# w_out as a Strassen product, x added by accumulating DMAs, eleven of gate_up's first products ahead

## The chip, the cores and the metric

One core of one Trainium2 chip runs the kernel. The metric is the device time of one execution in microseconds (us); the numbers shown are medians over runs. The profile beside it is one execution taken by the hardware profiler.

## The reference

One layer of a streaming encoder on x of 1024 tokens by 1024 channels, all in float32. What matters here, cut down:

```python
h = rmsnorm(x, norm_mix_pre)
proj = einsum("bsd,dn->bsn", h, w_in)            # q k v f, conv inputs, two gates
...                                              # branch A: gated short convolution
...                                              # branch B: forgetting attention, 8 heads
merged = sigmoid(gate_conv) * ya_d + sigmoid(gate_attn) * yb_d
m = einsum("bsd,de->bse", merged, w_out)         # 1024 x 1024 weights
x = x + rmsnorm(m, norm_mix_post)
h = rmsnorm(x, norm_ffn_pre)
gu = einsum("bsd,df->bsf", h, w_gate_up)         # 1024 x 5632
g, u = split(gu, 2)
f = einsum("bsf,fd->bsd", silu(g) * u, w_down)   # 2816 x 1024
x = x + rmsnorm(f, norm_ffn_post)
```

## The kernel before

**A product of matrices.** Each float32 operand is split into a rounded part `hi` (a copy on ScalarE, ACT) and the rest `lo` (a subtraction on VectorE, DVE). `mm3` then issues three matmuls, hi·hi, hi·lo and lo·hi, each 128 by 128 weights with 512 moving columns, into one PSUM bank. A `strassen` product takes a block of two by two blocks with seven block products instead of eight (Winograd's form): its sums of blocks are made by DVE on both operands, its results are combined by DVE from the banks `b1`, `b2`, `b3` into `c11`, `c12`, `c21`, `c22`. One block product here is 4 k-steps by 3 = 12 matmuls, a whole job is 84.

**The stages, in order.** Norm of x; the projections with w_in as 18 Strassen jobs; the attention, with the rest of branch A between its steps; branch B (`pbb`, 16 groups of 12 matmuls, whose results are gated and added into `um`, the transposed activations); w_out; gate_up as 22 Strassen jobs (f = 0 to 21); the down product (`pd`), the last norm and the output.

**w_out.** It is a plain product. `woh`/`wol` hold the whole weight matrix, split while `pbb` runs. `e_mm(st)` takes one tile of 128 tokens: two halves of 512 output columns, 8 k-steps, 3 matmuls each, into the bank `pm`. `e_norm(st)` follows one tile behind: sum of squares on ACT, a row scale `rms_scale` (six small DVE and ACT steps), the gain `gpo`, the addition of x (tile `xt`, loaded by the SP queue) on DVE, a POOL DMA that stores the new x in `x2_dram`, a second sum of squares and scale, the gain `gpr`, and eight transposes `tp` of 128x128 on TensorE (PE) that put the tile back into `um`.

**The first products.** Gate_up's Strassen jobs need activations of all tokens, but their first product and a half (`b1` over A11·B11 and A12·B21) only those of the first four tiles. So for f below `NPRE` these are done ahead (`f_first`): four of them before the last e_norm, the others between the groups of `h2_sums`, which form the sums of activations `hth` and `hch`. P1 and C11 are parked in `pre_dram` by POOL DMAs and loaded again (`c<-pre_dram`) when job f runs.

**What sets the order.** A scheduler places every instruction on its engine's queue at build time from dependences and priorities; the queues run in order. `strict` names engines whose instructions keep the order of the program. Pools have few buffers (4 `hi`, 3 `lo`, 3 `raw`, 1 `s4`, 2 `s4h`/`s4l`), so a load or a split also waits for the last reader of its buffer. A helper on line 76 records nearly all instructions, so rows are told apart by their tiles, not by lines; in the profile PE's bank of any Strassen product reads `b`, and its operands `hi`, `lo`, `s4h`, `s4l` and the activations' names.

Of the kernel before, what the change touches and what calls it, by code (L numbers as in the profile page):

```python
# [39 lines left out]
NPRE = 7  # L40
# [6 lines left out]
def block_kernel(  # L47
# [69 lines left out]

    def copy(o, a):
        nc.scalar.activation(o, a, AF.Copy)
# [16 lines left out]
    stat.tile([P, 24], F32, name="pad", bufs=1)  # L136
# [11 lines left out]
    pre_dram = [dpool.tile([2, P, NC], F32, name=f"pre_dram{f}") for f in range(NPRE)]  # L148
    ri_dram = [dpool.tile([2, S], F32, name=f"ri_dram{j}") for j in range(4)]
    sg_dram = [dpool.tile([2, P, S], F32, name=f"sg_dram{d}") for d in range(8)]  # L150
# [59 lines left out]
    av, av_close = pool("av")  # L210
    psa, psa_close = pool("psa", 4, space=PSUM)
# [82 lines left out]
    def turn(st, hn):  # L294
# [11 lines left out]
        if st < 4:  # L306
            if hraw is None:
                hraw = av.tile([P, KT, NC], F32, name="hraw")
# [36 lines left out]
        return [(b12h, b12l), bot], rest  # L345

# [37 lines left out]
    for st in range(ST):  # L384
# [5 lines left out]
        if st + 3 == ST:  # L390
            ax_close()
            w0, w0_close = pool("w0", side="right")
            r0 = w0.tile([P, KT, P], F32, name="r0")
            h0, l0 = (w0.tile([P, KT, P], F32R, name=n) for n in ("h0", "l0"))
            nc.sync.dma_start(r0, win[:, C_Q : C_Q + P].rearrange("(k p) m -> p k m", p=P))
            split(h0, l0, r0)
# [3 lines left out]

    av_close()
# [110 lines left out]
    def strassen(w, hb, psp, tmp, p1=None):  # L512
# [8 lines left out]
        prod(b2, w["S2"], hb[T2], True)  # L521
        c12 = t_(tmp, "c12")
# [301 lines left out]

    zts = {}
# [3 lines left out]
    for ij, (kind, j, _, _) in enumerate(jobs):  # L829
        if ij == 2:  # L830
            logf_pre = forget_sums()
# [55 lines left out]
        else:  # L887
# [286 lines left out]
    wo_pool, wo_close = pool("wo", side="right")  # L1174
    woh = wo_pool.tile([P, KT, D], F32R, name="woh")
    wol = wo_pool.tile([P, KT, D], F32R, name="wol")
# [25 lines left out]
    ha_pool, ha_close = pool("ha")  # L1202
    hah = ha_pool.tile([P, 2, 4, NC], F32R, name="hah")
    hal = ha_pool.tile([P, 2, 4, NC], F32R, name="hal")
    fp, fp_close = pool("f", 2)
    ep, ep_close = pool("e")
    gpo = bcast_row(norm_mix_post[0], ep, name="gpo")
    gpr = bcast_row(norm_ffn_pre[0], ep, name="gpr")

    def e_mm(st):  # L1210
        ss = slice(st * P, (st + 1) * P)
        mh, ml = hi_t(), lo_t()
        split(mh, ml, um[:, :, ss])
        pm = []
        for n in range(2):
            ns = slice(n * NC, (n + 1) * NC)
            ps = psm.tile([P, NC], F32, tag="mm", name="pm")
            for k in range(KT):
                mm3(
                    ps, (mh[:, k, :], ml[:, k, :]), (woh[:, k, ns], wol[:, k, ns]),  # L1220
                    k == 0, k == KT - 1,
                )
            pm.append(ps)
        return pm

    def load_xt(st):
        xt = z_tile("xt")
        nc.sync.dma_start(xt, x2d[st * P : (st + 1) * P, :])
        return xt

    def e_norm(st, pm):
        ss = slice(st * P, (st + 1) * P)
        xt = xts.popleft()
        if st + 1 < ST:
            xts.append(load_xt(st + 1))
        tt = ep.tile([P, D], F32, tag="t", name="tt", bufs=1)
        s2 = st_tile("s2", 2)
        for n in range(2):
            ns = slice(n * NC, (n + 1) * NC)
            nc.scalar.activation(tt[:, ns], pm[n], AF.Square, accum_out=s2[:, n : n + 1])  # L1240
        ssq = st_tile("ssq")
        add(ssq, s2[:, 0:1], s2[:, 1:2])
        rs = rms_scale(ssq)
        for n in range(2):
            ns = slice(n * NC, (n + 1) * NC)
            nc.vector.scalar_tensor_tensor(
                tt[:, ns], pm[n], rs, gpo[:, ns], op0=ALU.mult, op1=ALU.mult
            )
        add(xt, xt, tt)
        nc.gpsimd.dma_start(x2_dram[ss, :], xt)  # L1250
        ssq = st_tile("ssq")
        nc.scalar.activation(tt, xt, AF.Square, accum_out=ssq)
        rs = rms_scale(ssq)
        nc.vector.scalar_tensor_tensor(tt, xt, rs, gpr, op0=ALU.mult, op1=ALU.mult)
        for q in range(2):
            tp = psm.tile([P, 4, P], F32, tag="mm", name="tp")
            for k in range(4):
                kt = 4 * q + k
                nc.tensor.transpose(tp[:, k, :], tt[:, kt * P : (kt + 1) * P], ident)
            copy(um[:, 4 * q : 4 * q + 4, ss], tp)  # L1260
# [4 lines left out]
    def f_first(f):  # L1265
# [355 lines left out]
```

## Time and profile before

| what | value |
|---|---|
| time, median of 3 runs | 1350.11 us (1350.0 to 1350.78) |
| the profiled execution: its time, its span | 1350.04 us, 1348.2 us |
| PE busy, share of the span | 1328.5 us, 99% |
| DVE, ACT, POOL busy | 932.3, 535.2, 127.2 us |
| granted TensorE clock | 9 of 9 tenths in each of 40 slices |
| DMA moved | 186.36 MB, 138 GB/s |

The busy time of an engine is summed over its instructions' rows; for PE the rows' ends are modelled and neighbouring rows overlap, so the distance between starts tells its pace. The span is the time from the first to the last instruction of the profile. The execution's own time is 1.8 us longer than its span.

### The profile page before, as it was taken

The page shows a single profiled execution, that of the slowest core. Times are in us where ns is not written, and L with a number is a line of the kernel's source. Part 1 is how long each engine was busy: PE and PEld are TensorE (multiplying, and loading weights), DVE is VectorE, ACT ScalarE, POOL GpSimd, SP SyncE. Part 2 cuts the span into 40 slices and gives each one's busy share as a digit, 9 for nine tenths or more (in the row PEclk, how much of TensorE's full clock was granted, in tenths as well). Part 3 has the DMA queues.
Part 4 walks back from the last instruction along what each step waited for, and adds up shares of the span by engine and source line. Part 5 has one row for each costly group of instructions (what it writes and reads, how often), then busy time and mean ns, then how long its engine had stood idle before and what let it go on. Part 6 is the DMA issues. An engine that isn't in the chain of part 4 may idle for free.

```text
span 1348.2 us, 17709 instructions
## 1 busy us (share of the span) xinstructions
PE 1328.5 (99%) x6753; PEld 1098.9 (82%) x6753; DVE 932.3 (69%) x1445; ACT 535.2 (40%) x851; POOL 127.2 (9%) x252
## 2 busy tenths in 40 slices
PE   9999999999999999999999999999999999999997
PEld 7978888888887778788887788888888888888886
DVE  6974668754556766775669698776677766677585
ACT  6642222243345756613547232223222323444452
POOL 0001000011112112000002121100111011000000
PEclk9999999999999999999999999999999999999999
DMA  5332422333325444362235565332323236965541
GB/s 189 118 109 86 126 70 71 105 123 109 102 82 192 158 142 165 126 218 79 94 110 175 170 200 167 102 100 80 117 102 118 93 111 240 361 235 196 161 164 63
DMA packets 153256, 186.36 MB, mean 138 GB/s; under 512 B 9409, under 2 KB 106753, under 8 KB 153170
## 3 DMA queue, kind: packets, MB, share of 16 engines
q1 hardware_dynamic: 138434, 136.67, 32.4%
q0 software_dynamic: 14736, 48.54, 9.3%
q8 instruction: 53, 0.87, 0.3%
q14 instruction: 33, 0.27, 0.1%
HBM read 136.10 MB, written 49.09 MB: 137 GB/s over the span
## 4 chain that ended last, share of the span: by engine, by line
PE 58%; DVE 3%; DMA 2%; issue 1%; ACT 1%; POOL 0%; DVEq 0%; SPq 0%; POOLq 0%; ACTq 0%
PE b L76 28%; PE pd L76 15%; PE pm L76 5%; PE pbb L76 3%; PE pba L76 2%; PE po L76 1%; PE tps L76 1%; PE sp L76 1%; DMA pre_dram<-s 1%; DMA tk<-in_w_down_dram 1%; DVE tt L76 0%; DVE lo L76 0%; PE tp L76 0%; DMA pre_dram<-c 0%; ACT tt L76 0%
## 5 line engine op out<-in xcount | busy, mean ns | idle before, releaser
L76 DVE TENSOR_TENSOR c<-c,b 128x512 f32<-128x512 f32 x195 | 132.9, 682 | 91.4 <-PE b L76 72.3
L76 DVE TENSOR_TENSOR lo<-raw,hi 128x1024 fp32r<-128x1024 f32 (+1 forms) x93 | 112.0, 1204 | 83.1 <-PE b L76 68.8
L76 ACT ACTIVATE hi<-raw 128x1024 fp32r<-128x1024 f32 (+1 forms) x100 | 101.7, 1018 | 127.9 <-PE b L76 75.7
L76 PE MATMUL b<-hth,hi 128*128 128x512 f32 x352 | 137.3, 390 | 0.0
L76 PE MATMUL b<-hth,lo 128*128 128x512 f32 x352 | 137.0, 389 | 0.0
L76 PE MATMUL b<-htl,hi 128*128 128x512 f32 x352 | 136.9, 389 | 0.0
L76 ACT ACTIVATE hi<-sx 128x1024 fp32r<-128x1024 f32 x41 | 43.5, 1062 | 220.9 <-PE b L76 195.3
L76 PEld LDWEIGHTS b<-hth,hi 128*128 128x128 f32 x352 | 66.1, 188 | 14.6 <-DVE c L76 1.0
L76 PEld LDWEIGHTS b<-hth,lo 128*128 128x128 f32 x352 | 66.1, 188 | 13.8
L76 PEld LDWEIGHTS b<-htl,hi 128*128 128x128 f32 x352 | 66.1, 188 | 13.7
L76 DVE TENSOR_TENSOR lo<-sx,hi 128x1024 fp32r<-128x1024 f32 x41 | 50.2, 1224 | 33.6 <-PE b L76 31.4
L76 PE MATMUL b<-hah,hi 128*128 128x512 f32 x176 | 69.0, 394 | 1.2 <-ACT c L76 1.2
L76 PE MATMUL b<-hal,hi 128*128 128x512 f32 x176 | 68.5, 389 | 0.0
L76 PE MATMUL b<-hah,lo 128*128 128x512 f32 x176 | 68.4, 390 | 0.0
L76 DVE TENSOR_TENSOR sx<-raw 128x512 f32<-128x512 f32 x78 | 53.6, 688 | 19.1 <-DMA raw<-in_w_in_dram 9.0
L76 PE MATMUL pd<-hi,lo 128*128 128x512 f32 x160 | 62.3, 389 | 0.0
L76 PE MATMUL pd<-hi 128*128 128x512 f32 x160 | 62.0, 390 | 0.0
L76 PE MATMUL pd<-ghi 128*128 128x512 f32 x148 | 57.6, 390 | 0.0
L76 PE MATMUL pd<-glo,ghi 128*128 128x512 f32 x148 | 57.6, 389 | 0.0
L76 PE MATMUL pd<-ghi,glo 128*128 128x512 f32 x148 | 57.6, 389 | 0.0
L76 PE MATMUL b<-hT34h,hi 128*128 128x512 f32 x136 | 53.0, 390 | 0.4 <-DVE c L76 0.4
L76 PE MATMUL b<-hT34h,lo 128*128 128x512 f32 x136 | 52.9, 389 | 0.0
(368 smaller groups left out, 3359.9 us busy)
## 6 DMA issues: line engine op xcount, KB each, us to landing
raw<-in_w_gate_up_dram SPq DMA_DIRECT2D x51, 512.0 KB, 3.8
raw<-in_w_in_dram SPq DMA_DIRECT2D x35, 512.0 KB, 3.8
a_dramS<-um POOLq DMA_DIRECT2D x44, 256.0 KB, 2.8
a_dramA<-um POOLq DMA_DIRECT2D x33, 256.0 KB, 2.8
xt<-in_x_dram SPq DMA_DIRECT2D x16, 512.0 KB, 4.3
sg<-sg_dram SPq DMA_DIRECT2D x32, 256.0 KB, 4.6
graw<-a_dramS SPq DMA_DIRECT2D x14, 512.0 KB, 4.0
sg_dram<-c POOLq DMA_DIRECT2D x24, 256.0 KB, 2.3
```

Of the source, the lines that this page charges most:

```text
L76: ins = getattr(self.engine, name)(*args, **kw)
```

## The change

It has five parts.

1. **w_out by Strassen.** The tokens are taken as four pairs of tiles; each pair is a product of two by two blocks with 7 x 12 matmuls. For all four pairs the first product and a half come first (`first`, `second`; kept in `keeps`), then for each pair the other five products (`strassen`), `e_norm(i)` for two tiles at once, and `e_turn(i)`, its 16 transposes, placed in PE's queue behind the first product (S2) of pair i+2 for pairs 0 and 1, and within `f_first(0)` and `f_first(3)` for pairs 2 and 3. `sums` makes the sums of activations, those of pair 0 on POOL.
2. **w_out's weights.** Their seven block operands are formed and split during projection jobs 1 to 16 (`wo_load`: four loads of 128x128, four subtractions, one split of 128x896 each), stored in `wo_dram` by DMAs on ACT's queue one job later, and loaded as `x0` to `x5` (512 KB each, 28 loads) in `pbb` and after it.
3. **Gate_up's weights for the first products.** In projection jobs 1 to 11 one 128x1024 block each is loaded, split and stored in `pw_dram` (`pw_load`). `f_first` loads its `hi` and `lo` from there and splits nothing.
4. **NPRE 7 to 11.** Eleven first products are done ahead.
5. **x added by DMA.** `e_norm` writes the scaled tile into `x2t`; a POOL DMA adds x to it (`accum_op=add`), then an SP DMA stores it in `x2_dram`, and the second sum of squares reads it.

```diff
-NPRE = 7
+NPRE = 11
+    def pinned(call, *names):
+        was, strict[0] = strict[0], names
+        call()
+        strict[0] = was
...
-    def strassen(w, hb, psp, tmp, p1=None):
+    def strassen(w, hb, psp, tmp, p1=None, after=None):
...
         prod(b2, w["S2"], hb[T2], True)
+        if after is not None:
+            after()
         c12 = t_(tmp, "c12")
...
+    def wo_load(n):
+        k, c = divmod(n, 4)
+        r, h, l = w0_tiles()
+        for slot, (row, half) in enumerate(((k, 1), (k, 0), (4 + k, 0), (4 + k, 1))):
+            c0 = half * NC + c * P
+            nc.sync.dma_start(r[:, slot], wout_d[row * P : (row + 1) * P, c0 : c0 + P])
+        def cut():
+            for o, a, b in ((4, 0, 1), (5, 3, 4), (6, 3, 0), (7, 2, 5)):
+                sub(r[:, o], r[:, a], r[:, b])
+            split(h[:, 1:], l[:, 1:], r[:, 1:])
...
+    def pw_load(f):
+        r = t0_.tile([P, S], F32, tag="cb", name="rg", bufs=2)
+        h, l = (t0_.tile([P, S], F32R, tag="p", name=n, bufs=2) for n in ("hg", "lg"))
+        nc.sync.dma_start(kblk(r), kmaj(wgu[:, f * P : (f + 1) * P]))
...
     for ij, (kind, j, _, _) in enumerate(jobs):
+        for _, store in side.pop(ij - 1, ()):
+            pinned(store, "scalar")
+        if 0 < ij < len(jobs) - 1:
+            side[ij] = [wo_load(ij - 1)] + ([pw_load(ij - 1)] if ij <= NPRE else [])
...
+        for cut, _ in side.get(ij, ()):
+            pinned(cut, "vector", "scalar")
...
             sg = sg_tile()
             nc.sync.dma_start(sg, sg_dram[d][1, :, ns])
+            load_wo(*loads.pop(0))
...
-            if n == 0:
-                wr = flat(raw_t())
-                nc.sync.dma_start(wr, wout_d[d * P : (d + 1) * P, :])
-                split(woh[:, d, :], wol[:, d, :], wr)
+            if n and d == 1:
+                first_ops(0, [s4h_t(), s4h_t()], [s4l_t(), s4l_t()])
+                sums(0, s4_t())
...
+    def e_norm(i, c12, c21, c22):
+        qa, qb = qas[i], st2("qb")
+        for c, acc in ((c12, qb[:, 0:1]), (c21, qa[:, 1:2]), (c22, qb[:, 1:2])):
+            square(c, acc)
+        add(qa, qa, qb)
+        rs = scale2(qa)
...
+        for e, parts in enumerate((((n1, keeps[i][:, 1]), (n2, c12)), ((n1, c21), (n2, c22)))):
+            xt = xp[e]
+            for ns, c in parts:
+                nc.vector.scalar_tensor_tensor(
+                    xt[:, ns], c, rs[:, e : e + 1], gpo[:, ns], op0=ALU.mult, op1=ALU.mult
                 )
...
+            nc.gpsimd.dma_start(xt, x2d[rows_, :], accum_op=ALU.add)
+            nc.sync.dma_start(x2_dram[rows_, :], xt)
+            nc.scalar.activation(tt[e], xt, AF.Square, accum_out=ssq[:, e : e + 1])
+        rs = scale2(ssq)
...
-        add(xt, xt, tt)
-        nc.gpsimd.dma_start(x2_dram[ss, :], xt)
...
-    def f_first(f):
-        w, _ = prep_first(f_src(f)[0])
-        b1, p1 = strassen_first(w, hb, psm, fp)
+    def f_first(f, p1=None, after=None):
+        h1, l1 = hi_t(), lo_t()
+        for t, d in zip((h1, l1), pw_dram[f]):
+            nc.sync.dma_start(f32(flat(t)), d)
+        b1 = bank(psm, "b1")
+        prod(b1, (h1[:, LO], l1[:, LO]), hb[B11], True)
+        if after is not None:
+            after()
...
+    ops = rest_ops(0)
+    for i in range(PAIRS):
+        nxt = rest_ops(i + 1) if i + 1 < PAIRS else None
+        _, *cur = strassen(
+            ops, wob, psm, fe, keeps[i][:, 0], (lambda: e_turn(i - 2)) if i > 1 else None
+        )
+        e_norm(i, *cur)
...
+    f_first(0, p1_of(0), lambda: e_turn(2))
+    h2_sums(0)
+    f_first(1, p1_of(1))
+    h2_sums(1)
+    f_first(2, p1_of(2))
+    f_first(3, p1_of(3), lambda: e_turn(3))
...
+    for f in range(4, NPRE):
+        f_first(f)
```

**Where instructions stand now.** PE's queue at the first transposes of w_out's results. Before, the tile `tt_5835` (tokens 0 to 127) is turned behind all 48 matmuls of the next tile (`pm_5783` and `pm_5808`):

```order
L76 MATMUL pm_5808<-woh_5398,hi_5779 128x512
L76 MATMUL pm_5808<-wol_5399,hi_5779 128x512
L76 MATMUL pm_5808<-woh_5398,lo_5780 128x512
L76 MATMUL tp_5870<-ident_139,tt_5835 128x128 [waits DVE_49]
L76 MATMUL tp_5870<-ident_139,tt_5835 128x128 x3
L76 MATMUL tp_5876<-ident_139,tt_5835 128x128 x4
L76 MATMUL pm_5886<-woh_5398,hi_5882 128x512 [waits Activation_49]
```

In the changed kernel the same place is in pair 2: `b2_6524` is its S2, `tt_6351` and `raw_6121` are the two normed tiles of pair 0, `b3_6525` is pair 2's next product:

```order
L76 MATMUL b2_6524<-x2_5748,hi_6379 128x512 x2
L76 MATMUL b2_6524<-x2_5748,lo_6380 128x512
L76 MATMUL tp_6538<-ident_155,tt_6351 128x128 [waits DVE_49]
L76 MATMUL tp_6538<-ident_155,tt_6351 128x128 x3
L76 MATMUL tp_6544<-ident_155,tt_6351 128x128 x4
L76 MATMUL tp_6550<-ident_155,raw_6121 128x128 [waits DVE_49]
L76 MATMUL tp_6550<-ident_155,raw_6121 128x128 x3
L76 MATMUL tp_6556<-ident_155,raw_6121 128x128 x4
L76 MATMUL b3_6525<-x3_5749,hi_6383 128x512 [waits Activation_49]
```

Sixteen transposes now stand together, and in front of the rest of pair 2, where eight stood behind a whole tile.

ACT's queue in the same norm. Before, for the first tile: the sum of squares of the new x waits for DVE alone, and the copies from `tp` follow:

```order
L76 ACTIVATE tt_5835,s2_5836<-pm_5754 128x512 [waits PE_49]
L76 ACT_TABLE_LOAD
L76 ACTIVATE sq_5842<-va_5841 128x1 [waits DVE_49]
L76 ACTIVATE tt_5835,ssq_5856<-xt_5723 128x1024 [waits DVE_49]
L76 ACTIVATE sq_5859<-va_5858 128x1 [waits DVE_49]
L76 ACTIVATE hi_6203<-um_3496 128x1024 [waits PE_49,Activation_49]
L76 ACTIVATE um_3496<-tp_5870 128x4x128 [waits PE_49]
L76 ACTIVATE um_3496<-tp_5876 128x4x128 [waits PE_49]
```

In the changed kernel, for pair 0 (`DMASW` are semaphores of POOL's DMAs; `junk_6463` and `junk_6465` already belong to pair 1's norm):

```order
L76 ACTIVATE hi_6510<-um_3844 128x512 [waits PE_49]
L76 ACTIVATE hi_6510<-s3_6099 128x512
L76 ACTIVATE tt_6351,ssq_6354<-x2t_6352 128x1024 [waits DMASW3_49,DMASW7_49,DMASW2_49,DVE_49]
L76 ACTIVATE s4h_6520<-um_3844 128x512 [waits PE_49]
L76 ACTIVATE raw_6121,ssq_6354<-x2t_6353 128x1024 [waits DMASW3_49,DVE_49]
L76 ACTIVATE junk_6463,qb_6462<-c12_6407 128x512 [waits DVE_49,Activation_49]
L76 ACTIVATE sq_6366<-va_6365 128x2 [waits DVE_49]
L76 ACTIVATE hi_6514<-um_3844 128x1024 [waits PE_49]
L76 ACTIVATE junk_6465,qa_6105<-raw_6136 128x512 [waits DVE_49,Activation_49]
L76 ACTIVATE junk_6467,qb_6462<-c22_6421 128x512 [waits Activation_49]
L76 ACTIVATE um_3844<-tp_6538 128x4x128 [waits PE_49]
```

The squares of `x2t` wait for the accumulating DMAs, and pair 1's combining, squares and pair 3's splits stand between them and the transposes.

DVE's queue in a projection job. Before, the splits of the weights and the combining of the results:

```order
L76 TENSOR_TENSOR c12_2698<-c21_2682,b2_2684 128x512 [waits DMASW4_49,PE_49,Activation_49]
L76 TENSOR_TENSOR c22_2712<-c21_2682,b3_2685 128x512 [waits DMASW3_49,PE_49]
L76 TENSOR_TENSOR lo_2646<-raw_2643,hi_2645 128x1024 [waits PE_49]
L76 TENSOR_TENSOR lo_2656<-sx_2651,hi_2655 128x1024 [waits PE_49,Activation_49]
L76 TENSOR_TENSOR c22_2712<-c22_2712,b2_2684 128x512 [waits DVE_49]
```

In the changed kernel the sums and splits of w_out's weights (`r0`, `l0`) and of gate_up's (`lg`) stand in the same queue:

```order
L76 TENSOR_TENSOR r0_2431<-r0_2431 128x128 [waits DMAHW1_49]
L76 TENSOR_TENSOR s4l_2634<-s4_2631,s4h_2633 128x512 [waits Activation_49]
L76 TENSOR_TENSOR r0_2431<-r0_2431 128x128 [waits DMAHW4_49,DVE_49]
L76 TENSOR_TENSOR r0_2431<-r0_2431 128x128
L76 TENSOR_TENSOR r0_2431<-r0_2431 128x128 [waits DMAHW2_49,DVE_49]
L76 TENSOR_TENSOR c12_2666<-c21_2650,b2_2652 128x512 [waits PE_49]
L76 TENSOR_TENSOR c22_2680<-c21_2650,b3_2653 128x512 [waits PE_49]
L76 TENSOR_TENSOR l0_2433<-r0_2431,h0_2432 128x896 [waits DMAHW3_49,Activation_49]
L76 TENSOR_TENSOR lg_2440<-rg_2438,hg_2439 128x1024 [waits DMAHW7_49,Activation_49]
L76 TENSOR_TENSOR lo_2614<-raw_2611,hi_2613 128x1024 [waits PE_49]
L76 TENSOR_TENSOR c22_2680<-c22_2680,b2_2652 128x512 [waits DVE_49,PE_49]
```

Six instructions more stand in such a job, two of them ahead of the splits that PE needs next.

More of the change, by code (lines that the diff above doesn't have):

```diff
@@ L1226, in load_xt, with st2 @@
[L1226 to L1245, printed above, removed]
+    def st2(name, bufs=2):
+        return ep.tile([P, 2], F32, tag=name, name=name, bufs=bufs)
@@ new lines, in scale2, with square @@
+    def scale2(ssq):
+        return rms_scale(ssq, None, lambda n, w: st2(n), 2)
+    def square(src, acc):
+        junk = ep.tile([P, NC], F32, tag="junk", name="junk")
+        nc.scalar.activation(junk, src, AF.Square, accum_out=acc)
+    sx = wtile("sx", 1)
+    for i in range(1, PAIRS):
+        first_ops(i, hi_t(), lo_t())
+        sums(i, ep.tile([P, 4, P], F32, name="s3") if i == 3 else sx[:, 4 * i - 4 : 4 * i])
+    turned = []
+    qas = [st2("qa", PAIRS) for _ in range(PAIRS)]
+    b1s = {}
```

243 lines of the change are left out of this document (167 added, 76 removed).

## The prediction

> **What bounds the kernel.** I read the page's first two parts, then the chain of waits, then PE's rows at the stage that changes.
>
> ```profile
> span 1348.2 us, 17709 instructions
> PE 1328.5 (99%) x6753; PEld 1098.9 (82%) x6753; DVE 932.3 (69%) x1445; ACT 535.2 (40%) x851; POOL 127.2 (9%) x252
> L76 PE MATMUL b<-hth,hi 128*128 128x512 f32 x352 | 137.3, 390 | 0.0
> ```
>
> TensorE is the bound. But a matmul must not be priced at the 390 ns of its row: the rows overlap. The chain gives the pace, as long runs of matmuls with nothing between them:
>
> ```profile
> 567.59 43.52 PE pbb L76 x192
> 681.99 10.93 PE pm L76 x48
> 771.64 354.18 PE b L76 x1560
> ```
>
> 43.52 us / 192 and 354.18 / 1560 are both 0.227 us from start to start, and w_out's own 10.93 / 48 is 0.228. So a PE that never waits is paid by the number of matmuls at 0.2267 us, and what remains are its waits. From the end of the attention to the gate_up jobs these are few:
>
> ```profile
> PE b L76 <- DVE c L76: 2.1, 2, 1.5
> PE b L76 <- ACT c L76: 1.2, 1, 1.2
> PE tr L76 <- DVE ri L76: 0.7, 1, 0.7
> PE tp L76 <- DVE tt L76: 0.3, 1, 0.3
> ```
>
> These are the waits in 556 to 800 us: total, count, longest. `tr` belongs to the attention. The other 3.6 us are idle time after a modelled end; an interrupted pair of matmuls also loses the overlap of 0.39 - 0.227 = 0.16 us, which with two gaps of 0.2 us too small for the list makes about 4.6 us by starts.
>
> **Fewer matmuls.** The tile `pm` has three rows like this one, 384 matmuls:
>
> ```profile
> L76 PE MATMUL pm<-woh,hi x128: 389/389/481, 610.9 to 703.8; 128*128 128x512 f32 x128
> ```
>
> Four pairs by 7 products by 12 are 336. The first products of gate_up are only moved, and the 64 transposes stay. So 48 matmuls go: 48 x 0.2267 = 10.9 us (not 48 x 0.39 = 18.7).
>
> **Old waits that go.** The four waits above sit in front of code that is replaced: a norm tile late for its transposes, the last e_norm before f_first(4), the reload of P1 and C11 before the first gate_up jobs. I take all 4.6 us off and charge what is late next.
>
> **The norm of a pair, and its transposes.** This is the main new wait. The durations:
>
> ```profile
> L76 DVE SCALAR_TENSOR_TENSOR tt<-pm,r,gpo 128x512 f32<-128x512 f32 x14 | 9.9, 747 | 0.7
> L76 DVE SCALAR_TENSOR_TENSOR tt<-xt,r,gpr 128x1024 f32<-128x1024 f32 x7 | 9.0, 1285 | 0.2
> L76 DVE TENSOR_TENSOR sx<-um 128x512 f32<-128x512 f32 x1 | 0.7, 693 | 0.1
> L76 DVE TENSOR_SCALAR va<-ssq 128x1 f32<-128x1 f32 x14 | 2.2, 154 | 8.8 <-ACT tt L76 8.6
> L76 ACT ACTIVATE tt<-pm 128x512 f32<-128x512 f32 x14 | 8.2, 602 | 3.8 <-PE pm L76 3.8
> L76 ACT ACTIVATE tt<-xt 128x1024 f32<-128x1024 f32 x7 | 7.4, 1061 | 27.2 <-DVE xt L76 27.2
> L76 ACT ACTIVATION_READ_ACCUMULATOR tt<-pm 128x1 f32 x14 | 3.0, 213 | 0.0
> L76 ACT ACT_TABLE_LOAD x1 | 1.3, 1283 | 0.0
> ```
>
> Count from the last matmul of pair 0's fifth product. PE then has pair 1's 60 matmuls and pair 2's 12 of S2, 72 x 0.2267 = 16.3 us, until it stands at pair 0's transposes. Meanwhile DVE adds the last result (0.7), ACT squares the two last blocks (2 x 0.8) and loads a table (1.3), the scale takes six small steps of 0.15 to 0.2 us with their hand-overs (1.3), and two gains of 0.75 finish the first tile: POOL can issue at about 6.6 us, and for the second tile at 7.9. Landing takes L. Then ACT squares (1.06 + 0.18 us), but in the order of its queue: pair 3's split and pair 1's square stand in between (0.63 and 0.8), and DVE has pair 1's last addition and a split of 0.6 us ahead of the gains of 1.285 us. With L = 4.3 the second tile has landed at 12.2, is squared at 13.5, the scale (two engines, with 0.8 of pair 1's square and 1.3 of DVE's in between) ends at about 17.2, and the two tiles are ready at 18.6 and 19.9. PE waits from 16.3 to 18.6, turns eight blocks (0.9 us) and waits a little again: 2.5 us. The landing itself is nowhere in the trace of before, which has no accumulating DMA. The nearest rows:
>
> ```profile
> x_dram<-xt POOLq DMA_DIRECT2D x8, 512.0 KB, 2.9
> xt<-in_x_dram SPq DMA_DIRECT2D x16, 512.0 KB, 4.3
> DMA to landing us min/median/max: 2.9/2.9/7.3
> ```
>
> POOL's stores of the same 512 KB land in 2.9 us, the loads of the same rows of x in 4.3, and the slowest transfer of this tile took 7.3. An accumulation reads x as the load does, so I take 4.3, with 2.9 and 7.3 as ends. Per microsecond of L the wait grows by about one: 1.9 us (a floor, since the other work in both queues then sets it) to 5.5.
>
> The Trainium skill, "DMA: Bandwidth & Descriptors", section "Anatomy of one DMA — SWDGE (gpsimd) path", fits such a transfer as 2.0 us plus its bytes at 436 GB/s, which is an estimate of 3.2 us here; the 2.9 us of POOL's stores agrees. By it the four waits of this part would be about 2.5 us smaller in all and the sum 1341.0. That fit is for plain transfers, so I stay with the load's row.
>
> The same layout for the other pairs: pair 1's tiles are just in time (0.1; up to 3 at 7.3), pair 2's, turned in f_first(0), are late by 1.1 (0 to 4), pair 3's in f_first(3) by 1.7 (0.3 to 4.6). Pair 3's S4 product needs `c22` of an earlier bank released, behind four gains on DVE: 1.1 us (0 to 1.5). These are 6.5 us in all.
>
> **First products and their parking.** Eleven f_first issue 22 loads of 512 KB on SP; SP runs in order, and one load of f=7 stands behind raw loads that wait for DVE's sums. PE has 24 x 0.2267 = 5.4 us for each f_first, a load takes 3.8 in the row below, DVE nothing: 0.5 us (0 to 2).
>
> ```profile
> raw<-in_w_gate_up_dram SPq DMA_DIRECT2D x51, 512.0 KB, 3.8
> 745.55 4.80 DMA pre_dram<-c
> 751.27 3.07 DMA pre_dram<-s
> 756.68 0.47 PE L76 MATMUL b<-hch,s4h 128*128 128x512 f32 x1 [1.46 <-DVE c L76]
> ```
>
> The last three rows are the old case of the reload: POOL stores P1, waits, reloads, and PE's first S4 waits 1.46 us. In the new order the last f_first parks twice more just before the first job, and its `s4` is the buffer the job needs: the same wait, 1.5 us (0 to 2.2). The four jobs more that run with a reload cost nothing: in 772 to 900 us, where seven such jobs run, PE is never idle with DVE at 82%.
>
> **The projections.** Sixteen jobs get DVE work: four subtractions of 128x128 (between 0.15 us for 128x1 and 0.69 for 128x512; 0.3 by a straight line), a split of 128x896 (1.1) and, in eleven jobs, one of 128x1024 (1.22): 3.5 us. The cover is DVE's idle time, smallest in the conv jobs:
>
> ```profile
> core 0: us, PE busy (x) PEld busy (x) DVE busy (x) ACT busy (x) POOL busy (x), PEclk, DMA share, GB/s
> 147.00:166.10 19.10, 19.10 (x87) 15.73 (x86) 13.69 (x20) 5.42 (x7) 1.63 (x3) 1.00 0.58 167
> 261.90:281.00 19.10, 19.10 (x85) 15.79 (x85) 15.00 (x22) 7.33 (x9) 2.70 (x5) 1.00 0.47 152
> 772.00:900.00 128.00, 128.00 (x565) 105.57 (x564) 105.36 (x151) 37.23 (x47) 20.03 (x37) 1.00 0.45 146
> ```
>
> 15.0 + 3.5 = 18.5 of 19.1 us in the fullest, about 17.2 in the others: full, but under. A queue this full delays single splits that PE waits for; I take 0.4 us in all, and 4 as the upper end (0.5 in each of eight jobs). ACT has 12 us free per job; its four DMA issues (0.33 to 0.55 us on the other queues) wait for splits of a job before, so nothing stands behind them. In `pbb` the 28 loads replace eight splits; DVE and PE lose work or keep it: nothing.
>
> **The sum.** -10.9 (matmuls) - 4.6 (old waits) + 2.5 + 0.1 + 1.1 + 1.7 + 1.1 (pairs) + 0.5 + 1.5 (first products) + 0.4 (projections) = -6.6 us. The profiled execution took 1350.04 us, 0.07 below the median 1350.11, so the forecast is 1343.5. With no new wait at all it would be 1334.6; with L = 2.9, about 1340; with every wait of the pairs at its upper end, 1355.
>
> **Rivals.**
> (a) The turns are hidden: DVE and ACT are ahead of my layout, as in before, where of eight groups of transposes only one waits 0.3 us, and L is near 2.9. Then 2 to 4 us of waits remain: about 1338.
> (b) Slower: the accumulating DMA is slow. Each of the four turns gets a microsecond for each microsecond of L beyond 4.3, since POOL's landing stands on the chain of all of them: 6.6 us of gain are used up at L = 5.9, and 0.2% is lost at L = 6.6. At 7.3 the sum is 1355. For it: it reads and writes, and up to eight loads run beside it. Against it: the median rows, all under 5.
> By the Trainium skill, "TensorE: Matmul & The Clock Gate", section "Part 1: The HAM clock gate", an idle window of about 3.4 us halves the clock until some 3.4 us of work have passed. Then each gap longer than that would cost about 1.7 us more as an estimate; no gap of before is so long, and its clock is full throughout.
> (c) DVE saturates: the conv jobs' stall takes the upper end of 4 us, or more where a job's queue runs over. With 0.5 to 1 us in each of eight jobs the time is 1347 to 1351, no change.
>
> **How the numbers follow.** 0.2% of 1350 is 2.7 us, about what a measurement of this kernel can tell from no change. My sum (1341 to 1347.4): 0.52, at 1343.5. Rival (a), below 1341: 0.23. No change, by (c) or by L near 6 (1347.4 to 1352.8): 0.14. Slower by (b): 0.11. So faster is 0.75. The range reaches to (a) without its lower tail and through no change: 1336 to 1352.
>
> **What would show it.** PE's `pm` gone and 48 fewer 128x512 matmuls; the waits of `tp` for DVE's `tt` and `raw` at 2 to 3 us in pair 2, and one to two in the first f_first; the landing of `x2t<-in_x_dram` on POOL near 4.3; DVE at 17 to 18.5 of 19.1 us in the conv jobs with PE still full. I am wrong if the projections before 470 us end later by over a microsecond, if `x2t` lands after 6 us, or if PE waits in `pbb` for the loads of `x0` to `x3`.

## The result, and the profile after

The changed kernel takes 1400.74 us (median of 4 runs, 1397.32 to 1402.94) against 1350.22 us: 50.5 us slower, a ratio of 1.0371 with a 95% interval of 1.035 to 1.0393. The forecast was 1343.5. The page of the profiled execution:

```profile
span 1399.1 us, 18094 instructions
PE 1333.9 (95%) x6705; PEld 1098.6 (79%) x6705; DVE 965.3 (69%) x1522; ACT 550.8 (39%) x878; POOL 145.9 (10%) x272
PE   9999998889999999999886999999999999999997
PEclk9999999999999999999988999999999999999999
DMA  5357775777654543377358846653323325975541
```

The 48 matmuls are gone (6705 against 6753). PE's busy time has grown all the same, by 5.4 us, since some of the others run at half clock. And its row has two holes that the row of before had not: the seventh to ninth slice of 35 us (210 to 315 us, the projections) and the twentieth to twenty-second (665 to 770 us, w_out). In the second the page's row of the granted clock falls, too. Three stretches of after: the projections up to 502 us, w_out with the first products up to the first gate_up product that waits, and the part of gate_up behind it:

```profile
90.00:502.00 412.00, 387.04 (x1965) 313.43 (x1964) 275.40 (x459) 158.74 (x236) 43.70 (x86) 0.99 0.65 189
642.70:842.00 199.30, 174.96 (x761) 142.43 (x759) 111.18 (x197) 84.72 (x158) 22.87 (x37) 0.94 0.60 190
842.00:1177.00 335.00, 334.69 (x1475) 276.87 (x1476) 263.00 (x371) 96.14 (x122) 47.31 (x87) 1.00 0.41 134
```

The columns are length, busy time of PE, PEld, DVE, ACT, POOL, clock, DMA share and GB/s. Branch B begins at 599.2 us instead of 567.6 (its first matmul row at 599.0 and 567.4, which the experiments go by): the projections lost 31.6 us. From there to the same product of gate_up (842.3, before 771.6) it takes 39.1 us longer. That holds 48 more matmuls, since four first products (96) moved in and 48 went, 10.9 us; the waits by starts are 25.3 us where they were 4.6; the other 7.5 us are what is left over, and fit the half clock: four stretches of it, 23.9 us in all, in some 15.4 us of which PE works, at about half its pace. What follows is 19.8 us shorter. The four moved products are 96 x 0.2267 = 21.8 us. 31.6 + 39.1 - 19.8 = 50.9 us, the difference of the spans.

PE's waits, over the whole span (total, count, longest):

```profile
PE tp L76 <- DVE tt L76: 16.4, 3, 7.0
PE b L76 <- DVE c L76: 12.1, 10, 2.4
PE b L76 <- DVE lo L76: 10.8, 5, 3.9
PE b L76 <- ACT sx L76: 4.0, 1, 4.0
```

The first and last lines are the transposes and the product behind the last of them; of the other two 20.6 us lie in the projections. The chain of waits names the first group's cause, with the time from POOL's issue to the landing of two accumulations each:

```profile
682.91 2.12 DVE x2t L76 x4
685.03 9.68 DMA x2t<-in_x_dram x2
...
706.61 10.12 DMA x2t<-in_x_dram x2
```

and one hole of the projections, read over the four queues, gives the second. SP's queue, ACT's, DVE's, PE's rows around 290 to 309 us:

```profile
291.55 2.11 SPq L76 DMA_DIRECT2D r<-in_w_out_dram  x4
293.76 0.97 SPq L76 DMA_DIRECT2D rg<-in_w_gate_up_dram  x1
294.83 13.70 SPq L76 DMA_DIRECT2D raw<-in_w_in_dram  x2
...
290.34 0.38 ACTq L76 DMA_DIRECT2D wo_dram<-h  x1
291.56 0.42 ACTq L76 DMA_DIRECT2D wo_dram<-l  x1
292.07 0.59 ACTq L76 DMA_DIRECT2D pw_dram<-hg  x1
295.04 0.34 ACTq L76 DMA_DIRECT2D pw_dram<-lg  x1
...
305.58 0.69 DVE L76 TENSOR_TENSOR sx<-raw 128x512 f32<-128x512 f32 x1 [7.84 <-DMA raw<-in_w_in_dram]
...
308.19 0.79 PE L76 MATMUL b<-hT12h,lo 128*128 128x512 f32 x1 [3.86 <-DVE lo L76]
308.78 0.63 PE L76 MATMUL b<-hT12h,hi 128*128 128x512 f32 x1
309.21 0.63 PE L76 MATMUL b<-hT12l,hi 128*128 128x512 f32 x1
```

Four stores of 0.45 to 0.5 MB and five added loads are issued within 5 us; w_in's `raw`, issued among them at 294.83, is there at 305.5 (its row holds two loads, the second of 308.16). DVE stands still for 7.84 us, in order, with the split that PE waits for behind it. The median landing of these loads in 147 to 320 us, before and after, of those that the profile could time:

```profile
raw<-in_w_in_dram SPq DMA_DIRECT2D x18, 512.0 KB, 3.8
...
raw<-in_w_in_dram SPq DMA_DIRECT2D x16, 512.0 KB, 7.0
```

This hole is one of eight between 147 and 340 us in which DVE waits over 3 us for a `raw`, 38.1 us in all (the profile puts three of them down to "issue"). Each of these loads arrives 6.1 to 10.8 us after its issue, and what they take beyond 3.8 us adds up to 32.5 of the 38.1 us. The rest, 0.7 us a wait, is the size of the waits before. So these loads are late because they land late, not because SP issues them late. And after the gap in PE's rows the next matmuls start 0.43 us apart instead of 0.227: half clock.

### The profile page after: what moved, and what is told of

Read it like the earlier page. It is cut to its first block, busy times and chain, and to the rows that moved or that the text cites. A ratio compares the mean times of both kernels' runs of the same rounds, so it can differ in the third digit from the quotient of the medians.

```text
span 1399.1 us, 18094 instructions
## 1 busy us (share of the span) xinstructions
PE 1333.9 (95%) x6705; PEld 1098.6 (79%) x6705; DVE 965.3 (69%) x1522; ACT 550.8 (39%) x878; POOL 145.9 (10%) x272
## 4 chain that ended last, share of the span: by engine, by line
PE 51%; issue 4%; DMA 3%; DVE 2%; ACT 2%; POOL 1%; DVEq 0%; POOLq 0%; SPq 0%; ACTq 0%
PE b L76 27%; PE pd L76 15%; PE pbb L76 3%; PE pba L76 2%; DMA x2t<-in_x_dram 2%; PE po L76 1%; PE tps L76 1%; PE sp L76 1%; DMA raw<-in_w_gate_up_dram 1%; DMA tk<-in_w_down_dram 1%; POOL pre_dram L76 0%; DVE x2t L76 0%; ACT junk L76 0%; ACT x L76 0%; DVE lo L76 0%
## 5 line engine op out<-in xcount | busy, mean ns | idle before, releaser
L76 PE MATMUL b<-x,hi 128*128 128x512 f32 x1232 | 383.6, 392 | 4.3 <-ACT sx L76 4.0
L76 PEld LDWEIGHTS b<-x,hi 128*128 128x128 f32 x1232 | 231.5, 189 | 54.9 <-ACT sx L76 4.7
L76 PE MATMUL b<-x,lo 128*128 128x512 f32 x616 | 240.9, 391 | 1.7 <-DMA lo<-pw_dram 1.7
L76 DVE TENSOR_TENSOR lo<-raw,hi 128x1024 fp32r<-128x1024 f32 x82 | 98.6, 1203 | 61.9 <-PE b L76 49.7
L76 PEld LDWEIGHTS b<-x,lo 128*128 128x128 f32 x616 | 116.3, 189 | 26.6 <-DMA lo<-pw_dram 2.1
L76 DVE TENSOR_TENSOR lo<-sx,hi 128x1024 fp32r<-128x1024 f32 (+1 forms) x43 | 51.5, 1199 | 39.1 <-PE b L76 37.1
L76 PE MATMUL b<-hT12h,lo 128*128 128x512 f32 x136 | 55.2, 406 | 10.9 <-DVE lo L76 10.8
L76 PE MATMUL b<-hT12h,hi 128*128 128x512 f32 x136 | 54.2, 399 | 0.0
L76 PE MATMUL b<-hT12l,hi 128*128 128x512 f32 x136 | 54.1, 398 | 0.0
L76 PE MATMUL b<-hT34l,hi 128*128 128x512 f32 x136 | 53.1, 390 | 0.0
```

The source lines that it names most:

```text
L76: ins = getattr(self.engine, name)(*args, **kw)
```

## The experiments

All but one are compared with the kernel before on the same chip (1349.9 to 1350.6 us). "Branch B" is the start of its first matmul row, 567.4 us before and 599.0 after. Where a kernel stores or computes something that nobody reads, its edit says so.

**Which queue? `stores_pool`, `loads_pool`, `side_split_pool`.** Three theories for the projections, each with its own queue or engine relieved:

```diff
-                nc.scalar.dma_start(pw_dram[f][hl], f32(t))   # and wo_dram
+                nc.gpsimd.dma_start(pw_dram[f][hl], f32(t))
```

> The four stores of the split weights (w_out's and gate_up's) in each projection job are issued from POOL's queue instead of ACT's; all else as in the changed kernel, whose branch B begins at 599.2 us, 31.6 later than before. Theory A (ACT's queue: the stores wait there for DVE's splits and for semaphores of earlier DMAs, and the splits hi and s4h that TensorE needs stand behind them): more than half of the 31.6 us comes back, branch B begins before 584 and the time falls to about 1380. Theory B (SP's queue: the loads of w_out's blocks wait for their one buffer, and w_in's loads stand behind them): little comes back, under 8 us. Theory C (DVE is simply full): nothing comes back.

1396.34 us (1.0345, 1.033 to 1.0361); branch B 594.8.

```diff
-            nc.sync.dma_start(r[:, slot], wout_d[...])
+            nc.gpsimd.dma_start(r[:, slot], wout_d[...])
```

> The four 128x128 loads of w_out's blocks in each projection job are issued from POOL's queue instead of SP's; the stores stay on ACT's queue. Theory A (stores block ACT's queue): under 8 us of the 31.6 come back. Theory B (these loads wait for their one buffer in SP's queue, with w_in's loads behind them): more than half comes back, the loads of raw from w_in land in time and DVE's 22 us of waiting for them between 147 and 320 us fall to about 5. Theory C (DVE full): nothing.

1397.13 us (1.035, 1.0332 to 1.0367); branch B 596.3.

```diff
-                sub(r[:, o], r[:, a], r[:, b])
-            split(h[:, 1:], l[:, 1:], r[:, 1:])
+                nc.gpsimd.tensor_tensor(r[:, o], r[:, a], r[:, b], op=ALU.subtract)
+            copy(h[:, 1:], r[:, 1:])
+            nc.gpsimd.tensor_tensor(l[:, 1:], r[:, 1:], f32(h[:, 1:]), op=ALU.subtract)
```

> The four subtractions and the lo parts of the added splits in the projections are computed on POOL instead of DVE; DMAs and queues stay. Theory C (DVE is full, 15.0 of 19.1 us in a conv job plus 3.5): most of the 31.6 us comes back, since DVE is as loaded as before and POOL was busy 44 of 412 us. Theories A and B (queues): POOL's subtractions take longer than DVE's, so the stores and the release of the buffer come later, and the stage stays as long or grows by up to 20 us.

1415.58 us (1.049, 1.0474 to 1.0506); branch B 615.0. None of the three moves gives the stage back: a relieved queue returns 3 to 4 us of 31.6, and taking DVE's volume away while the transfers stay makes it 16 us worse. But two of them brought a new wait along. With the stores on POOL's queue DVE waits less for `raw`, and instead, between 147 and 340 us, 13.1 us for `ya_dram<-ot` and 9.8 for `pw_dram<-lg`; with the splits on POOL, ACT waits 18.4 us for its `lg`. So these two don't price ACT's queue or DVE's volume by themselves. `loads_pool` is cleaner: there each of the eight late loads of `raw` is issued as soon as its buffer is free, and still takes 5.0 to 11.3 us, which makes 36.1 of DVE's 41.0 us of waits. There it is not SP's queue order that makes them late.

**The accumulation: `x_load`.**

```diff
+        for e in range(2):
+            nc.sync.dma_start(xp[e], x2d[(2 * i + e) * P : (2 * i + e + 1) * P, :])
...
-                    xt[:, ns], c, rs[:, e : e + 1], gpo[:, ns], ...
+                    tt[e][:, ns], c, rs[:, e : e + 1], gpo[:, ns], ...
-            nc.gpsimd.dma_start(xt, x2d[rows_, :], accum_op=ALU.add)
-            nc.sync.dma_start(x2_dram[rows_, :], xt)
+            add(xt, xt, tt[e])
+            nc.gpsimd.dma_start(x2_dram[rows_, :], xt)
```

> x is loaded into the norm's tile by SP ahead of time, added by DVE, and the sum is stored by POOL, as in the kernel before; no accumulating DMA; the rest as in the changed kernel. If the landing of the accumulating DMA makes the transposes late: the waits of the transposes for the normed tiles fall from 16.4 us to under 5, the half clock near 700 to 770 us goes, and the time falls by 18 to 25 us to about 1378. If the two queues' other work sets these waits (DVE and ACT in order): the two additions of 1.2 us come on top and the time falls by less than 5 us or rises.

1382.1 us (1.0244, 1.0225 to 1.0262), 18.6 us less, at the edge of what was expected. No wait of a transpose for a normed tile is left; waits of 11 us by starts remain from branch B on, at other places, and the half clock comes back behind two of them. Branch B begins at 600.3.

**Splits or transfers? `proj_all`, `proj_splits`, `proj_dmas`.** On the kernel before: the change's work in the projections, whole and in two halves.

```diff
+        if 0 < ij < len(jobs) - 1:
+            side[ij] = [wo_load(ij - 1)] + ([pw_load(ij - 1)] if ij <= 11 else [])
...
+        for cut, _ in side.get(ij, ()):
+            pinned(cut, "vector", "scalar")
```

> The kernel before, with only the change's work in the projections added (loads, subtractions, splits and stores of w_out's and gate_up's weights, in the same places of the queues); nothing reads what is stored, and w_out stays a plain product. If the projections' 31.6 us are this work's own: branch B begins near 599 us instead of 567.6 and the time is about 1381. If they come from the changed kernel's other layout (buffers, order): under 1360.

1387.2 us (1.0275, 1.024 to 1.031); branch B 601.9: the delay is this work's own (4.3 us of it lie before 147 us, where the changed kernel has none).

```diff
+    def cut_only(wide):              # from r0, h0 as they lie
+        for o, p_, q_ in ((4, 0, 1), (5, 3, 4), (6, 3, 0), (7, 2, 5)):
+            sub(r0[:, o], r0[:, p_], r0[:, q_])
+        split(h0[:, 1:], l0[:, 1:], r0[:, 1:])
+        if wide:
+            split(h0, l0, r0)
```

> The kernel before, with the added subtractions and splits alone on DVE and ACT, on data that already lies in the tiles: no loads, no stores, and no wait but for each other. Theory C (DVE's volume, 3.5 us in a job): most of the 31.6 us appears, 1375 or more. Theory of the transfers (w_in's loads land later beside the added traffic, and DVE had no slack for that): under 5 us, 1350 to 1355, as my sum had it.

1352.1 us (1.0013, 1.0002 to 1.0024); branch B 568.9. All the added DVE and ACT work costs 1.5 us there.

```diff
+    def loads_only(n, wide):         # into r0 and a tile of their own
+    def stores_only(n, wide):        # from h0, l0, on ACT's queue
```

> The kernel before, with the added loads and stores alone (from and to tiles that nobody else uses, so that they wait for no split). Theory of the transfers: the landing of raw from w_in rises from 3.8 to about 7 us, DVE waits for it, and 10 us or more of the 31.6 appear. Theory C: under 3 us. If neither this run nor the one with the splits alone shows more than 8 us, the delay comes from the two together: waits of the loads and stores for the splits within the in-order queues, on a DVE with no time to catch up.

1365.26 us (1.0113, 1.0083 to 1.0142); branch B 583.1. This is 15.7 us, ten times what the splits cost, but not at the places of after: with nothing to wait for, the loads ran ahead and made gaps near 75 and 102 us (the second of 4.5 us), with half clock behind them. 12.8 us are lost before 156 us; between 147 and 320 us PE lost only 2.4 us. DVE's busy time and the transfers in 147 to 320 us, in the two runs:

```profile
147.00:320.00 173.00, 173.00 (x765) 143.24 (x764) 143.27 (x219) 66.15 (x77) 11.44 (x21) 1.00 0.34 101
147.00:320.00 173.00, 170.65 (x752) 140.09 (x751) 115.87 (x164) 45.16 (x55) 11.01 (x21) 1.00 0.68 207
```

The first is the splits alone: DVE at 143 of 173 us and PE never idle. The second is the transfers alone, with 207 GB/s, as much as in after (202). There, too, DVE waits for late loads, up to 6.3 us at a time, but it is busy for only 116 of 173 us and makes most of it up. So neither half alone shows the delay at its place.

**The landing: `landing`.** A kernel of its own that times transfers, each kind four times in one execution, and computes nothing of the block.

> A kernel of its own that computes nothing of the block: it times transfers of 512 KB of x into a tile, each kind four times, one at a time: SP load, POOL load, POOL accumulation, two POOL loads at once, two accumulations at once, and one of each beside six SP loads. If the accumulation itself is slow: 6 us or more alone against about 3 for POOL's plain load, and about 10 for two at once. If it is slow only beside other traffic: about 3 to 4 alone, 8 or more beside the six loads, and the plain POOL load suffers the same.

Issue to landing, in us:

```profile
sp_one<-in_x_dram SPq DMA_DIRECT2D x4, 512.0 KB, 3.3
pool_one<-in_x_dram POOLq DMA_DIRECT2D x4, 512.0 KB, 3.6
acc_one<-in_x_dram POOLq DMA_DIRECT2D x4, 512.0 KB, 5.2
acc_two_b<-in_x_dram POOLq DMA_DIRECT2D x4, 512.0 KB, 6.8
pool_busy<-in_x_dram POOLq DMA_DIRECT2D x4, 512.0 KB, 3.5
acc_busy<-in_x_dram POOLq DMA_DIRECT2D x4, 512.0 KB, 6.7
```

Between the two theories: an accumulation of 512 KB alone takes 1.6 us longer than the same plain load; beside six loads it takes 6.7 us, while a plain load in the same place, just ahead of the six, takes 3.5. The second of two is at 6.8 (a plain one 4.6).

**Both queues relieved: `x_load_dma_pool`.** `x_load` with the edits of `stores_pool` and `loads_pool`.

> The run with x loaded and added by DVE, and with both queue waits of the projections taken away at once: w_out's block loads and all stores of split weights are issued by POOL (gate_up's block loads stay on SP). If the two queue waits hide each other, so that each alone gave back only 3 to 5 of the 31.6 us: 15 us or more come back together, branch B begins before 585 us and the time is near 1366. If what delays TensorE is a DVE without idle time waiting for w_in's loads that land late beside the traffic: the two add up to about 8 us, 1374.

1409.24 us (1.0428, 1.041 to 1.0445); branch B 627.5. Both theories missed: POOL's queue became the next one that stands in order, DVE now waits for the block loads in it (147 to 340 us), and the stage is 28 us longer still:

```profile
DVE r L76 <- DMA r<-in_w_out_dram: 25.2, 6, 7.2
DVE ot L76 <- DMA ya_dram<-ot: 15.3, 2, 7.8
```

**Without gate_up's weights: `no_pw`.** `x_load`, and:

```diff
-            side[ij] = [wo_load(ij - 1)] + ([pw_load(ij - 1)] if ij <= NPRE else [])
+            side[ij] = [wo_load(ij - 1)]
...
-        for t, d in zip((h1, l1), pw_dram[f]):
-            nc.sync.dma_start(f32(flat(t)), d)
+        w, _ = prep_first(f_src(f)[0])
```

> The run with x loaded and added by DVE, and without gate_up's weights in the projections: the eleven first products load and split their block themselves, as the seven did before. In jobs 1 to 11 this takes away 1.2 of 3.5 us of DVE, 0.5 MB of loads and 1 MB of stores each; w_out's work stays. If DVE's volume and the traffic together make the delay: branch B begins 15 us or more earlier than 600 us and the time is near 1366 or less; the first products may wait a few microseconds for their splits. If w_out's single buffer and its queue order make it: under 8 us.

1372.52 us (1.0163, 1.0148 to 1.0178). Branch B at 570.4: of the 31.6 us 28.6 are gone (29.9 against `x_load`), and w_out's part costs 3. The time fell by only 10, since the first products now wait, 14.3 us for `hi` and 3.7 for `lo`: the `raw` buffers that their loads need are held by others. Two of these loads, at 668.6 and 707.4 us, wait for transposes of w_out's normed tiles; the one in front of the longest wait, 7.2 us, is held back for 20.6 us, until DVE has split the sums of activations that lie in its buffer.

**Other jobs: `light`.** On `no_pw`, with the stores on POOL's queue. Projection jobs 4 to 9 are those of the convolution, 10 to 17 those of the gates.

```diff
+        if ij in (1, 2, 3) or 10 <= ij < len(jobs) - 1:
+            side[ij] = [wo_load(units.popleft())]
+        def between():                       # behind S2 of jobs 10 to 15
+            (cut, store), = side.pop(ij)
+            pinned(cut, "vector", "scalar")
+            store()
+            side[ij] = [wo_load(units.popleft())]
```

> As the run without gate_up's weights in the projections, and w_out's sixteen units are moved out of the conv jobs (15.0 of 19.1 us of DVE already used) to jobs 1 to 3 and, two to a job, to the gate jobs 10 to 16 (under 10 of 19.1 us used); their stores are issued by POOL. If the fullness of DVE in the conv jobs is needed for the delay: branch B begins within 5 us of 567.6, and the time is 1350 to 1355, since the w_out stage with loaded x still waits some 11 us. If the transfers alone delay w_in's loads: the delay moves to the gate jobs and the time stays above 1362.

1418.69 us (1.0508, 1.0492 to 1.0523). The conv jobs run without a gap, but branch B begins at 616.5. This says nothing on the theories: with two units in a job and one buffer, DVE's split waits for the store of the one before:

```profile
DVE l L76 <- DMA wo_dram<-l: 40.7, 7, 7.8
```

**Gate_up's part taken apart: `pw_splits`, `pw_dmas`.** On `no_pw`, whose branch B begins at 570.4.

```diff
-        return lambda: split(h, l, r), store
+        return lambda: split(h, l, f32(hB11[0])[:, 0:2]...), store     # no load, store() does nothing
```

> The run without gate_up's weights in the projections (branch B begins at 570.4 us, w_out's work there all the same), with only the splits of such weights put back: one hi on ACT and one lo of 128x1024 on DVE in jobs 1 to 11, from a tile that always lies there; no loads, no stores; the first products split for themselves. If DVE's time is what counts: 15 of the 28.6 us between 570.4 and 599.0 or more come back, branch B after 585. If the transfers count, or only both together: branch B before 576.

1374.1 us (1.0174, 1.0154 to 1.0194); branch B 571.8.

```diff
-                nc.scalar.dma_start(pw_dram[f][hl], f32(t))
-        return lambda: split(h, l, r), store
+                nc.scalar.dma_start(pw_dram[f][hl], r)                 # the loaded tile
+        return lambda: None, store
```

> The same run with only the transfers of gate_up's weights put back: 512 KB loaded and twice 512 KB stored in jobs 1 to 11, the stores taken from the loaded tile, so that they wait for no split; no added DVE or ACT time. If the transfers count (w_in's loads land later and a DVE that w_out's part has filled cannot make it up): branch B after 585. If only DVE's time or both together count: before 576.

1388.2 us (1.0278, 1.0258 to 1.0299); branch B 589.4. So of the 28.6 us the splits alone make 1.4, the transfers alone 19.0, and the two together the rest. The 19.0 are not only late landings, though: the tile `rg` is stored as it was loaded, so its next load waits in SP's queue for that store (40.6 us in 147 to 320, which after does not have), with loads of `raw` behind it. Of DVE's 36.6 us in nine waits for `raw` (147 to 340 us) 24.0 are landing beyond 3.8 us; the rest is 1.4 us a wait, where after has 0.7. DVE's waits for w_in's loads in 147 to 320 us, in the kernel before, in `no_pw` and in `pw_dmas`:

```profile
DVE sx L76 <- DMA raw<-in_w_in_dram: 5.3, 8, 1.0
...
DVE sx L76 <- DMA raw<-in_w_in_dram: 14.1, 7, 3.6
...
DVE sx L76 <- DMA raw<-in_w_in_dram: 28.7, 8, 6.5
```

DVE waited for these loads before the change already: they were just in time, with no slack. At 14.1 us of waits DVE still keeps PE fed; at 28.7 it does not. (In after this row has 21.9 us, and 12.4 more that the profile puts down to "issue"; in `pw_dmas` these are 13.1.)

**Five first products: `pw5`, `pw5_act`.** `x_load`, gate_up's weights in jobs 1 to 3, 10 and 11 only; the stores on POOL's queue, then on ACT's.

```diff
+            side[ij] = [wo_load(ij - 1)] + ([pw_load(PWJ.index(ij))] if ij in PWJ else [])
+        if f < len(PWJ):
...
+        else:
+            w, _ = prep_first(f_src(f)[0])
```

> x loaded and added by DVE; gate_up's weights prepared for five first products only, in jobs 1 to 3, 10 and 11, outside the conv jobs; the other six split for themselves; all stores of split weights on POOL. If the delay needs the conv jobs' full DVE beside those transfers: branch B begins near 570, and since the first five first products have their weights in time, the waits for hi and lo in them (18 us without prepared weights) go and the time is 1349 to 1354. If it does not: branch B after 580 and the time above 1360.

1366.39 us (1.0117, 1.0101 to 1.0134), branch B 579.3: close to the second case. POOL's queue is among the causes, with DVE waiting 6.7 us for `ya_dram`.

> As pw5, with the stores back on ACT's queue. There POOL's queue held the stores of the conv results behind them (DVE waited 6.7 us for ya_dram) and branch B began at 579.3. If that is what was left of the delay: branch B begins near 572 and the time is about 1359; w_out's stage, with 14 us of waits of half a microsecond and more, still keeps it above the kernel before. If the transfers of five jobs outside the conv jobs still count: branch B after 577, time above 1363.

1363.34 us (1.0095, 1.0078 to 1.0111), branch B 577.9, the worse of the two cases. The conv jobs now run full:

```profile
147.00:281.00 134.00, 133.93 (x591) 110.18 (x590) 106.50 (x170) 41.20 (x48) 7.08 (x13) 1.00 0.60 159
```

Three gaps of 0.7 to 2.8 us lie at 308 to 331 us, just behind jobs 10 and 11, which carry gate_up's transfers and have a DVE that is busy for 24.7 of 38 us (268 to 306). The load of `raw` issued at 294.56, as soon as its buffer was free, took 9.2 us, and DVE waited 5.96 us for it. So a full DVE is not needed for the delay: two loads that land 5 and 7 us late are enough. It is the fastest of the variants and still 12.8 us behind the kernel before.

**The same place without accumulation: `x_plain_pool`.**

```diff
-            nc.gpsimd.dma_start(xt, x2d[rows_, :], accum_op=ALU.add)
+            nc.gpsimd.dma_start(xt, x2d[rows_, :])
```

The load writes over the scaled tile, so the sum leaves out w_out's part.

> The changed kernel, with POOL's accumulating DMA replaced by a plain POOL load of the same rows into the same tile at the same place; the normed tile's part of the sum is left out. If the accumulation makes the landing long: it falls from a median of 7.8 us to below 5, the transposes' waits of 16.4 us fall to a third, and the time falls by about 15 us to 1385. If POOL's queue or the traffic beside it makes it long: the landing stays above 7 us and the time near 1400.

1388.44 us (1.0281, 1.0261 to 1.0302): 12.3 us less than after. The median landing in 640 to 850 us, of after and of this run:

```profile
x2t<-in_x_dram POOLq DMA_DIRECT2D x8, 512.0 KB, 7.8
...
x2t<-in_x_dram POOLq DMA_DIRECT2D x8, 512.0 KB, 5.2
...
PE tp L76 <- DVE tt L76: 5.2, 2, 3.0
```

The accumulation makes 2.6 of the 7.8 us; the place, with w_out's loads beside it, makes 1.6 (5.2 against 3.6 alone). The transposes' waits fall from 16.4 us to 5.2.

## Why the prediction was wrong, point by point

- **Fewer matmuls, 10.9 us.** Right: 48 fewer, and the pace of 0.2267 us stayed wherever nothing waited and the clock was full.
- **The projections, 0.4 us (0 to 4).** This step failed most: 31.6 us. Its DVE volume was sized right (the splits alone cost 1.5 us on the kernel before, DVE at 143 of 173 us). What I left out was what the added 2 MB and more of each job do to w_in's loads: they land 6.1 to 10.8 us after their issue instead of 3.8. I priced transfers by what stands behind them in their own queue, and never asked which other transfer lands later. The row was there: DVE's 5.3 us of waits for `raw`, none over 1.0. A transfer that is waited for already has no slack, whatever the engine's busy share says. "Nothing stands behind" ACT's stores was wrong, too (up to 6.5 us of waits in front of `hi`); moving the stores to POOL's queue gave only 4.2 us, but with new waits there, so that ACT's share is not known. Rival (c) named the stage, with another mechanism and a fifth of the size.
- **L = 4.3 us.** Wrong: a median of 7.8, and 9.7 to 10.1 for the pairs on the chain, over my upper end of 7.3. The mechanism of rival (b) held, the landing on the chain of every turn; the step that failed is the choice of a plain load's row for an operation that no row showed. The layout behind it was, if anything, too slow: with `x_plain_pool`'s 5.2 us, for which my slope of one gives some 9 us over the four turns, the waits for a normed tile are 2.2 and 3.0 us, 5.2 in all.
- **The pairs' S4 wait, 1.1 us.** Absent in after, where the late transposes took its place; with x loaded it is there, 0.9 and 1.8 us.
- **Old waits, 4.6 us off, and the reload, 1.5 us.** Two of the four old waits came back, as 1.75 and 0.83 us before the first gate_up jobs. The reload was priced right; the second was not charged.
- **The first products' loads, 0.5 us.** One wait for `lo` from `pw_dram`, 1.7 us: within its range of 2.
- **The clock.** The chance of gaps long enough was tied to rival (b) alone. In after gaps lower it in both stages, and about 7.5 us of the w_out stage and 4 of the projections (20 matmuls, 0.2 us longer each) go to work at half clock. The Trainium skill, "TensorE: Matmul & The Clock Gate", section "Part 1: The HAM clock gate", says that an idle window of about 3.4 us halves the clock, and that it takes about as long of sustained work to come back. The gap of 4.0 us before 308.19 agrees with the first part; the clock stayed at half for 6.8 us, for 14 matmuls, twice as long as my estimate in (b) had it. The last section has shorter gaps.

Two of the signs of being wrong that the prediction named came true: the projections ended later by far more than a microsecond, and `x2t` landed after 6 us.

What stays open: splits and transfers together cost 8 us more than the sum of the two (28.6 against 1.4 + 19.0), and part of the 19.0 are late issues that after does not have. That a DVE with less idle time cannot catch up after a late load fits, and `proj_dmas` points the same way, but no run shows it by itself. Nor is it known which of the added transfers make `raw` late, the loads just in front of it in SP's queue or the stores on ACT's. Nor was a version found that beats the kernel before: even with the projections at +3 us (`no_pw`), the waits that w_out's new order leaves, 11 us and more, are as large as the 10.9 us of matmuls.

## What to carry to other kernels

Moving work into a stage whose engines have idle time adds transfers to it as well; before pricing the work, look for loads that are waited for there already, by however little, because they will be the ones that land later. An operation that no row shows, such as an accumulating DMA, is measured alone first, and its range is not closed at the slowest plain transfer. A store or load that waits in an in-order queue is moved from one queue to the next at a price: three of the four such moves here made the next queue the late one (`stores_pool`, `x_load_dma_pool`, `pw5`; not `loads_pool`).

## What the runs showed of the hardware

- An accumulating DMA of 512 KB from DRAM into SBUF takes 5.2 us alone and 6.7 beside six loads, where a plain POOL load takes 3.6 and 3.5; POOL's issue of it takes 0.87 us instead of 0.55.
- The granted clock halves after gaps shorter than I had allowed for. In the run with x loaded, PE stood idle for 2.17 us, and the matmuls behind it start 0.43 us apart:

```profile
729.05 0.39 PE L76 MATMUL b<-x,lo 128*128 128x512 f32 x1
731.61 0.82 PE L76 MATMUL b<-x,hi 128*128 128x512 f32 x2 [2.17 <-ACT sx L76]
732.23 0.63 PE L76 MATMUL b<-x,lo 128*128 128x512 f32 x1
732.65 1.06 PE L76 MATMUL b<-x,hi 128*128 128x512 f32 x2
```

  By the rule of the Trainium skill quoted above ("TensorE: Matmul & The Clock Gate", "Part 1: The HAM clock gate"), an idle window of about 3.4 us, this gap would have been free; the measurement decides. The length of a gap alone does not tell: one of 1.82 us in `stores_pool` (before 253.73) had matmuls 0.43 us apart behind it, one of 2.66 us in after (before 216.71) had none.
- What does tell, in these traces, is a grid. The falls and rises of the granted clock within a run lie whole multiples of 3.41 us apart. Cut by this grid into stretches of 3.41 us, the 15 runs in which the clock fell have, between 60 and 1150 us, 75 stretches at full clock in which PE was idle for 1.95 us or more (gaps over 0.2 us counted): the clock was half in the next stretch each time. Of the 128 with 0.9 to 1.74 us idle none was followed by half clock, of the nine in between four. So a little over half a stretch of idle time was enough here, and whether a gap of 1.8 to 3.4 us costs anything depends on where it falls.
